# An SSM layer on one core: the first decays' arithmetic moved up, z in half blocks, evictions and residual adds given priority

## The chip, the cores and the metric

The kernel runs as one program on one core of a Trainium2 chip. The metric is the device time of one execution in microseconds (us), a median over several runs. The engines are named as in the profile: PE is the matmul engine and PEld its weight loads, DVE the vector engine, ACT the scalar (activation) engine, POOL the general engine, SP the engine whose queue issues most of the transfers. Matmuls read SBUF and write PSUM, which has eight banks here; a bank can be written again only when what lay in it has been read out.

## The reference, cut to what matters

A two-layer encoder works on 256 prompt tokens and 8 streams of 16 tokens, so 384 tokens of width 1024. Layer 0 is a short convolution beside attention, then a feed-forward block with a convolution. Layer 1, which the change is about, is a state-space (SSM) mixer, followed by another feed-forward block. Its core:

```python
proj = h @ w_in
z, xbc, dt_raw = jnp.split(proj, [D_INNER, D_INNER + CONV_DIM], axis=-1)
xbc, new_conv = causal_dwconv(xbc, conv_state, conv_w, conv_b)
xbc = jax.nn.silu(xbc)
xs, bm, cm = jnp.split(xbc, ...)
dt = jax.nn.softplus(dt_raw + dt_bias);  a = -jnp.exp(a_log)
...
cum = jnp.cumsum(dtc * a, axis=2)
decay = jnp.exp(jnp.where(tri, cum[q] - cum[s], -jnp.inf))
mix = cb[..., None] * decay * dtc            # cb = C B^T within a chunk
y_intra = jnp.einsum('bcqsgr,bcsgrp->bcqgrp', mix, xc)
...
y = (y + d_skip * xs) * jax.nn.silu(z)
y = rms_norm(y in 4 groups, norm_w);  out = y @ w_out;  x = x + out
```

There are 32 heads of 64 in 4 groups, a state of 128, and a convolution over 4 tokens.

## The kernel before, in words

Every product is made of three matmuls (`three`, line 421): weights and activations are each split into a high and a low part, and high x high, high x low and low x high are added in one PSUM bank. The weights come as a stream of tiles of 128 x 1024 in the order of their use. `Weights.take` (line 385) hands out the next columns, and has the tile after the current one made: a transfer on SP's queue, a copy on ACT (`wh`, the high part), a subtraction on DVE (`wl`, the low part). Each of raw, `wh` and `wl` has three buffers, so a tile's `wh` waits until the matmuls of the tile three before it are done.

In the SSM layer PSUM's banks are shared out as three for products (`pmm`) and five for the rest (`paux`). The channels x, B and C come out of `conv4` (line 938) one tile of 128 channels at a time: 24 matmuls of 384 columns into a `pmm` bank (`xbc`), the eviction into `pad` as two DVE multiplications by the norm's factor `R` (lines 946 and 947: 256 and 128 columns), then one ACT and three DVE steps of the convolution (`c`) and a Silu on ACT.

The layer then works through four groups g. `Group.within` (line 1083) makes the states `S` and the part of y within a chunk: per block b a matmul pair `S`, which needs `xw` (POOL, from the turned x), and 32 small matmuls `y`, which need `xdt` (DVE, from the turned x) and the decays `td`. The turned x, `xt`, is x transposed on PE and copied out by ACT, three copies (`turn_x`, line 1006). `decays` (line 1019) is a generator in two parts: the first issues four transfers that spread the cumulated sums over the partitions; the second, after its `yield`, runs 16 Relus and 4 exponentials on ACT. `Group.__init__` (line 1040) multiplies each of the four results by `CB` on DVE.

`project_z` (line 1137) makes z for 512 channels: three `pmm` banks, one for each 128 tokens, over eight slices (kt) of the input width; it is a generator with one step for each three matmuls of 512 columns, 24 steps in all, which the main loop spreads between other work (`steps`). Two kts make one weight tile. `add_out` (line 1197) makes the output projection of the group before: eight products `op` of twelve matmuls, two for each weight tile, each in a `pmm` bank, and each added to the residual stream X by DVE (`residual`, line 518).

What sets the order: all of it is straight-line code. On PE the instructions of this layer keep the order in which they are written (`T.keep`). On the other engines the framework chooses each engine's order when it compiles: it runs a timing model and takes, among the instructions that the model holds ready, the one with the best priority. Priority is the order of writing, except that what is written under `tc.high_priority()` is treated as if it stood at the start of the program. So before the change these go ahead: the making of weight tiles, the `CB` products, the copy of `S` (named `S0` in the code), the adds of y, the scaling of `yi`, and the copies of the turned y. The order is then fixed, and on the chip each engine runs its queue strictly in that order.

Of the kernel before, what the change touches and what calls it, by code (L numbers as in the profile page):

```python
# [14 lines left out]
ALU = mybir.AluOpType  # L15
# [5 lines left out]
KT = 8  # L21
# [209 lines left out]
def build(nc, tc, d, stop=None):  # L231
# [35 lines left out]
    def pmm(name):  # L267
        return psum["mm"].tile([P, 512], F32, tag="mm", name=name)

    def paux(name):  # L270
        return psum["aux"].tile([P, 512], F32, tag="aux", name=name)
# [11 lines left out]
    def prc(name, i):  # L283
        o = COL[name] + i
        return prm[:, o:o + 1]
# [6 lines left out]
    R = cp.tile([P, NT], F32, name="R")  # L292
# [6 lines left out]
    def tt(out, a, b, op, eng=None):  # L299
        (eng or V).tensor_tensor(out=out, in0=a, in1=b, op=op)  # L300

    def stt(out, a, s, b, op0, op1):
        V.scalar_tensor_tensor(out=out, in0=a, scalar=s, in1=b, op0=op0, op1=op1)  # L303

    def act(out, a, f, **kw):
        S.activation(out, a, f, **kw)  # L306
# [92 lines left out]
    W = Weights()  # L399
# [21 lines left out]
    def three(out, ah, al, bh, bl, start, stop):  # L421
        T.matmul(out, lhsT=ah, rhs=bh, start=start, stop=False)
        T.matmul(out, lhsT=ah, rhs=bl, start=False, stop=False)
        T.matmul(out, lhsT=al, rhs=bh, start=False, stop=stop)
# [3 lines left out]
    def run(gen):  # L428
        while True:
            try:  # L430
                next(gen)
            except StopIteration as e:
                return e.value
# [15 lines left out]
    def fm_group(ps, mh, ml, kts, start=True, stop=True):  # L449

        kts = list(kts)
        for i, kt in enumerate(kts):
            wh, wl = W.take()
            three(ps[:, :NT], wh, wl, mh[:, kt, :], ml[:, kt, :],
                  start and i == 0, stop and i == len(kts) - 1)
            yield

    def tm_group(name):

        ps = [pmm(f"{name}{b}") for b in range(3)]  # L460
        for kt in range(KT):
            wh, wl = W.take(512)
            for b in range(3):
                o = slice(b * P, (b + 1) * P)
                three(ps[b], Hh[:, kt, o], Hl[:, kt, o], wh, wl, kt == 0, kt == KT - 1)
                yield
        return ps
# [3 lines left out]
    def small_group(w, n, name, pool):  # L471


        ps = paux(name)
        for kt in range(KT):
            strip = slice(32 * (kt % 4), 32 * (kt % 4) + 32)
            T.matmul(ps[strip, :NT], lhsT=w[:, kt, :], rhs=X[:, kt, :], start=kt < 4, stop=kt >= 4)
        t = pool.tile([P, NT], F32, tag="sq", name=name + "s", bufs=2)
        act(t, ps[:, :NT], AF.Copy)
        ps = paux(name + "t")  # L480
        for b in range(3):
            T.matmul(ps[:, b * n:(b + 1) * n], lhsT=t[:, b * P:(b + 1) * P], rhs=C("hsel")[:, 0:n], start=True, stop=True)
        return ps


    def norm_tile(kt, gain, layer, pool):
        g = prc(gain, 8 * layer + kt)
        act(Hh[:, kt, :], X[:, kt, :], AF.Copy, scale=g)
        stt(Hl[:, kt, :], X[:, kt, :], g, f32(Hh[:, kt, :]), ALU.mult, ALU.subtract)
        if kt == 0:  # L490
            act(acc, X[:, kt, :], AF.Square)
        else:
            sq = pool.tile([P, NT], F32, tag="sq", name="sq", bufs=2)
            act(sq, X[:, kt, :], AF.Square)
            tt(acc, acc, sq, ALU.add)
# [22 lines left out]
    def residual(mt, ps):  # L518
        tt(X[:, mt, :], X[:, mt, :], ps[:, :NT], ALU.add)

    def tok_s(ap):
        return ap.rearrange("p (b t) -> p b t", t=LB)

    def padded(t, w):

        return t[:, 0:w + 256], t[:, w + 256:w + 256 + NB * (LB + w)].rearrange("p (b t) -> p b t", t=LB + w)
# [18 lines left out]
    ps = paux("warm")  # L545
# [55 lines left out]
    def to_features(src, name, fill=None):  # L601

        ps = paux(name)
        for i in range(4):
            T.transpose(ps[:, i * P:(i + 1) * P], src[:, i * P:(i + 1) * P], ident)
        if fill:
            fill(4)
        return ps.rearrange("p (k t) -> p k t", t=P)


    ps = small_group(wsm[:, 0], 8, "f", e1)
# [9 lines left out]
    ps = paux("lfT")  # L621
# [19 lines left out]
    for b in range(3):  # L641
        ps = to_features(q[:, b, :], "qT")
# [8 lines left out]
    for b in range(3):  # L651
        ps = to_features(k[:, b, :], "kT")
# [4 lines left out]
    ps = run(tm_group("v"))  # L657
# [125 lines left out]
    for b0 in range(0, NB, 3):  # L783
        nb = min(3, NB - b0)
        ps = paux("ss")
# [29 lines left out]
    ps = paux("pn")  # L815
# [7 lines left out]
    for j in range(2):  # L823
# [14 lines left out]
        ps = paux("aoT")  # L838
# [12 lines left out]
    for m0 in (0, 4):  # L851
        ps = ops if m0 == 0 else [pmm("op") for _ in range(4)]
# [82 lines left out]
    def t512(tag, bufs=2, shape=(P, 512)):  # L935
        return o1.tile(list(shape), F32, tag=tag, name=tag + "_", bufs=bufs)

    def conv4(i, out):

        ps = pmm("xbc")  # L940
        yield from fm_group(ps, Hh, Hl, range(KT))
        pad = o1.tile([P, 411], F32, tag="pad", name="pad4")
        pp_, ps_ = padded(pad, 3)
        G.memset(pp_[:, 0:3], 0.0)
        G.tensor_copy(ps_[:, :, 0:3], sts[:, i])
        tt(pp_[:, 3:], ps[:, 0:256], R[:, 0:256], ALU.mult)
        tt(ps_[:, :, 3:], tok_s(ps[:, 256:384]), tok_s(R[:, 256:384]), ALU.mult)
        G.tensor_copy(osm[:, i, 0:3], pp_[:, 256:259])
        G.tensor_copy(osm[:, i, 3:27].rearrange("p (b t) -> p b t", t=3), ps_[:, :, 16:19])
        c = o1.tile([P, 411], F32, tag="c", name="c4")  # L950
        act(c[:, 0:408], pad[:, 0:408], AF.Identity, scale=prc("cvs", i), bias=prc("cvsb", i))
        for t in (1, 2, 3):
            stt(c[:, 0:408], pad[:, t:408 + t], prc("cvs", 24 * t + i), c[:, 0:408], ALU.mult, ALU.add)
        act(out[:, 0:256], c[:, 0:256], AF.Silu)
        act(tok_s(out[:, 256:384]), c[:, 259:411].rearrange("p (b t) -> p b t", t=19)[:, :, 0:16], AF.Silu)


    ps = small_group(wsm[:, 1], 32, "dt", o1)
# [11 lines left out]
    def conv_x(g, i):  # L970
        out = t512("xf", 4, (P, NT))
        run(conv4(4 * g + i, out))
        return out

    def conv_bc(which, g):
        out = t512("BC"[which], 1 + which, (P, NT))
        run(conv4(16 + 4 * which + g, out))
        return out
# [158 lines left out]
    def project_z():  # L1137

        ps = [pmm(f"z{b}") for b in range(3)]
        for k0 in (0, 4):  # L1140
            ws = [W.take(512) for _ in range(4)]
            for b in range(3):
                o = slice(b * P, (b + 1) * P)
                for i, (wh, wl) in enumerate(ws):
                    three(ps[b], Hh[:, k0 + i, o], Hl[:, k0 + i, o], wh, wl, k0 + i == 0, k0 + i == KT - 1)
                    yield
        zs = t512("zs", 1, (P, 3, 512))
        for b in range(3):
            act(zs[:, b, :], ps[b], AF.Silu, scale=r[:, b:b + 1])
        return zs  # L1150
# [46 lines left out]
    def add_out(yh, yl, factor):  # L1197
        for m0 in range(0, 8, 2):
            ws = [W.take(256) for _ in range(4)]
            for m in range(2):  # L1200
                ps = pmm("op")
                for kt in range(4):
                    wh, wl = ws[kt]
                    o = slice(m * P, (m + 1) * P)
                    three(ps[:, :NT], wh[:, o], wl[:, o], yh[kt], yl[kt], kt == 0, kt == 3)
                    yield
                if factor is None:
                    residual(m0 + m, ps)
                else:
                    o = t512("xdt", 3, (P, NT))  # L1210
                    tt(o, ps[:, :NT], factor, ALU.mult)
                    tt(X[:, m0 + m, :], X[:, m0 + m, :], o, ALU.add)
                    norm_tile(m0 + m, "g_ffn", 1, o1)
# [15 lines left out]
    bc_ = turn_bc(0, Bn, Cn)  # L1229
    xs.append(conv_x(0, 3))  # L1230
    ps = paux("cT")
# [9 lines left out]
    ps = paux("E")  # L1241
# [11 lines left out]
    decs = decays(0)  # L1253
    next(decs)
    Bn, Cn = conv_bc(0, 1), conv_bc(1, 1)
    nx = [conv_x(1, 0)]
    tjd = t512("h0", 8, (P, 32, LB))
    tt(tjd, dA[:, 64:96].unsqueeze(2).broadcast_to([P, 32, LB]),
       C("Tj").unsqueeze(1).broadcast_to([P, 32, LB]), ALU.mult)
    ps = paux("sgS")  # L1260
# [1 line left out]
    act(decS, ps, AF.Exp)  # L1262

    xt = turn_x(xs)
    grp = Group(0, run(decs), bc_)
    grp.take(xt)
    xs = [*nx, conv_x(1, 1), conv_x(1, 2)]
    grp.skip()
# [1 line left out]
    for g in range(4):  # L1270
# [3 lines left out]
        if gate:  # L1274
            for b in range(3):
                gate.turn(b)
            op = add_out(*gate.y2, None)
        if last:
            break
        decs = run(decays(g + 1))  # L1280
        xs.append(conv_x(g + 1, len(xs)))
        grp.inter(1)
        bc_ = turn_bc(g + 1, Bn, Cn)
# [22 lines left out]
        grp = nxt  # L1306
# [22 lines left out]
    steps(op)  # L1329
    nc.gpsimd.dma_start(out=d["o_sm"], in_=osm)  # L1330
    run(add_out(*gate.y2, gate.factor()))
    T.keep = False
    r = norm_factor(o1)
# [22 lines left out]
```

## Time and profile before

| | |
|---|---|
| time, median of 3 runs | 1062.48 us (1061.84 to 1063.17) |
| time of the profiled execution | 1065.19 us |
| its span (first to last instruction) | 1063.4 us |
| SSM layer's groups, in the span | about 490 to 780 us |
| PE busy in the span | 1039.9 us (98%) |
| DVE, ACT, POOL busy | 739.8, 511.6, 104.4 us |

Times in a row of the profile count from the start of the span. A timeline's row gives the start, the length, the engine, the line, the operation with output and inputs, and a count; in brackets stands the idle time of the engine before it and what ended that. Most lines are those of helpers: L300 is a DVE tensor-tensor operation, L303 a DVE scalar-tensor-tensor, L306 an ACT activation, L240 a matmul.

### The profile page before, as it was taken

The page shows a single profiled execution, that of the slowest core. Times are in us where ns is not written, and L with a number is a line of the kernel's source. Part 1 is how long each engine was busy: PE and PEld are TensorE (multiplying, and loading weights), DVE is VectorE, ACT ScalarE, POOL GpSimd, SP SyncE. Part 2 cuts the span into 40 slices and gives each one's busy share as a digit, 9 for nine tenths or more (in the row PEclk, how much of TensorE's full clock was granted, in tenths as well). Part 3 has the DMA queues.
Part 4 walks back from the last instruction along what each step waited for, and adds up shares of the span by engine and source line. Part 5 has one row for each costly group of instructions (what it writes and reads, how often), then busy time and mean ns, then how long its engine had stood idle before and what let it go on. Part 6 is the DMA issues. An engine that isn't in the chain of part 4 may idle for free.

```text
span 1063.4 us, 16718 instructions
## 1 busy us (share of the span) xinstructions
PE 1039.9 (98%) x6316; PEld 969.7 (91%) x6316; DVE 739.8 (70%) x1361; ACT 511.6 (48%) x855; POOL 104.4 (10%) x339
## 2 busy tenths in 40 slices
PE   9999999999999999999899999899999999999998
PEld 6788799999999999989678888787989999999998
DVE  6967657777777734458989979868987776665331
ACT  5444335444444433346968668364544444443221
POOL 0030010100000000013313112210001100000000
PEclk9999999999999999999999999999999999999999
DMA  7542434344343443435555463553533434434541
GB/s 261 170 158 81 160 112 128 126 122 137 119 132 127 130 136 119 126 108 167 188 187 190 159 198 130 190 179 103 179 125 120 127 120 123 133 122 135 151 136 43
DMA packets 50329, 150.31 MB, mean 141 GB/s; under 512 B 5992, under 2 KB 8312, under 8 KB 50248
## 3 DMA queue, kind: packets, MB, share of 16 engines
q1 hardware_dynamic: 44360, 136.78, 40.9%
q10 hardware_dynamic: 4608, 8.39, 2.1%
q0 software_dynamic: 1280, 4.06, 1.0%
q8 instruction: 50, 0.82, 0.3%
q14 instruction: 31, 0.25, 0.1%
HBM read 135.81 MB, written 13.40 MB: 140 GB/s over the span
## 4 chain that ended last, share of the span: by engine, by line
PE 38%; DVE 13%; ACT 3%; issue 2%; DMA 0%; ACTq 0%; DVEq 0%
PE fg L240 9%; PE fd L240 9%; PE fa L240 8%; PE z L240 4%; PE xbc L240 3%; DVE wl L300 2%; DVE c L303 2%; PE op L240 2%; DVE wl L303 1%; DVE X L300 1%; ACT wh L306 1%; PE y L240 1%; DVE pad L300 1%; PE S L240 0%; ACT L306 0%
## 5 line engine op out<-in xcount | busy, mean ns | idle before, releaser
L300 DVE TENSOR_TENSOR wl<-raw,wh 128x1024 fp32r<-128x1024 f32 (+1 forms) x205 | 252.5, 1232 | 140.6 <-ACT wh L306 140.1
L306 ACT ACTIVATE wh<-raw 128x1024 fp32r<-128x1024 f32 (+1 forms) x205 | 216.0, 1054 | 225.0 <-PE fd L240 95.0
L240 PE MATMUL fg<-Hh,wh 128*128 128x384 f32 x352 | 119.0, 338 | 1.0 <-DVE pad L300 1.0
L240 PE MATMUL fa<-Hl,wh 128*128 128x384 f32 x352 | 119.3, 339 | 0.6 <-DVE Hl L303 0.6
L240 PE MATMUL fg<-Hl,wh 128*128 128x384 f32 x352 | 119.2, 339 | 0.0
L240 PE MATMUL fa<-Hh,wl 128*128 128x384 f32 x352 | 119.0, 338 | 0.0
L240 PE MATMUL fg<-Hh,wl 128*128 128x384 f32 x352 | 119.0, 338 | 0.0
L240 PE MATMUL fa<-Hh,wh 128*128 128x384 f32 x352 | 118.9, 338 | 0.0
L240 PE MATMUL fd<-hh,wh 128*128 128x384 f32 x352 | 118.3, 336 | 0.0
L240 PE MATMUL fd<-hh,wl 128*128 128x384 f32 x352 | 118.3, 336 | 0.0
L240 PE MATMUL fd<-hl,wh 128*128 128x384 f32 x352 | 118.3, 336 | 0.0
L303 DVE SCALAR_TENSOR_TENSOR c<-pad,prm,c 128x400 f32<-128x400 f32 (+1 forms) x160 | 101.9, 645 | 7.9 <-ACT c L306 6.2
L240 PEld LDWEIGHTS fg<-Hh,wh 128*128 128x128 f32 x352 | 66.2, 188 | 1.3 <-ACT R L306 1.3
L240 PEld LDWEIGHTS fa<-Hl,wh 128*128 128x128 f32 x352 | 66.1, 188 | 1.1 <-DVE Hl L303 0.9
L240 PE MATMUL xbc<-Hh,wh 128*128 128x384 f32 x192 | 65.9, 343 | 0.7 <-DVE X L300 0.7
L240 PEld LDWEIGHTS fa<-Hh,wl 128*128 128x128 f32 x352 | 66.2, 188 | 0.1
L240 PEld LDWEIGHTS fg<-Hl,wh 128*128 128x128 f32 x352 | 66.2, 188 | 0.1
L240 PEld LDWEIGHTS fg<-Hh,wl 128*128 128x128 f32 x352 | 66.2, 188 | 0.1
L240 PEld LDWEIGHTS fa<-Hh,wh 128*128 128x128 f32 x352 | 66.1, 188 | 0.1
L240 PEld LDWEIGHTS fd<-hh,wh 128*128 128x128 f32 x352 | 66.2, 188 | 0.0
L240 PEld LDWEIGHTS fd<-hl,wh 128*128 128x128 f32 x352 | 66.2, 188 | 0.0
L240 PEld LDWEIGHTS fd<-hh,wl 128*128 128x128 f32 x352 | 66.2, 188 | 0.0
(737 smaller groups left out, 2108.1 us busy)
## 6 DMA issues: line engine op xcount, KB each, us to landing
raw<-w SPq DMA_DIRECT2D x219, 512.0 KB, 3.5
kc<-kc SPq DMA_DIRECT2D x8, 256.0 KB, 3.5
vc<-vc SPq DMA_DIRECT2D x8, 256.0 KB, 3.0
X<-x SPq DMA_DIRECT2D x8, 192.0 KB, 4.7
o_y<-X SPq DMA_DIRECT2D x8, 192.0 KB, 2.8
o_v<-vt POOLq DMA_DIRECT2D x3, 256.0 KB, 2.5
o_k<-kraw POOLq DMA_DIRECT2D x3, 256.0 KB, 3.3
cst<-cst SPq DMA_DIRECT2D x1, 617.0 KB, 5.9
```

The lines of the kernel that those rows point to most:

```text
L240: ins = nc.tensor.matmul(*a, **kw)
L300: (eng or V).tensor_tensor(out=out, in0=a, in1=b, op=op)
L303: V.scalar_tensor_tensor(out=out, in0=a, scalar=s, in1=b, op0=op0, op1=op1)
L306: S.activation(out, a, f, **kw)
```

## The change

Four edits, no work added or removed:

1. The two DVE multiplications that evict a channel's PSUM bank into `pad` are written under high priority.
2. z is computed in four blocks of two kts instead of two blocks of four: in each, the three banks in turn take six matmuls instead of twelve, and the weights are taken for two kts at a time. The number of steps and of matmuls is the same.
3. The add of an output product to X is written under high priority, where the product needs no factor (the first three groups; the last one's has a factor and is unchanged).
4. For group 0, the second part of `decays` (16 Relus, 4 exponentials) is run right after the first channel of the next group, ahead of the product `tjd`, the exponential `decS` and the turning of x, instead of behind them.

```diff
@@ conv4 @@
-        tt(pp_[:, 3:], ps[:, 0:256], R[:, 0:256], ALU.mult)
-        tt(ps_[:, :, 3:], tok_s(ps[:, 256:384]), tok_s(R[:, 256:384]), ALU.mult)
+        with tc.high_priority():
+            tt(pp_[:, 3:], ps[:, 0:256], R[:, 0:256], ALU.mult)
+            tt(ps_[:, :, 3:], tok_s(ps[:, 256:384]), tok_s(R[:, 256:384]), ALU.mult)
@@ project_z @@
-        for k0 in (0, 4):
-            ws = [W.take(512) for _ in range(4)]
+        for k0 in range(0, KT, 2):
+            ws = [W.take(512) for _ in range(2)]
             for b in range(3):
                 o = slice(b * P, (b + 1) * P)
                 for i, (wh, wl) in enumerate(ws):
@@ add_out @@
                 if factor is None:
-                    residual(m0 + m, ps)
+                    with tc.high_priority():
+                        residual(m0 + m, ps)
@@ main @@
     nx = [conv_x(1, 0)]
+    decs = run(decs)
     tjd = t512("h0", 8, (P, 32, LB))
...
     xt = turn_x(xs)
-    grp = Group(0, run(decs), bc_)
+    grp = Group(0, decs, bc_)
```

## The prediction

> **What bounds the kernel now.** I read the share of busy time first, then PE's waits in the SSM layer, then the load of the other engines and the granted clock there, and last the timelines around the longest waits.
>
> ```profile
> PE 1039.9 (98%) x6316; PEld 969.7 (91%) x6316; DVE 739.8 (70%) x1361; ACT 511.6 (48%) x855; POOL 104.4 (10%) x339
> ```
>
> PE sets the time: whatever is to be won is PE's idle time, and the time in which it runs at a lower clock. No matmul is removed, so the whole question is how many of PE's waits in this layer go. They are these (the columns are total, number, longest):
>
> ```profile
> PE y L240 <- DVE td__4915 L300: 4.6, 1, 4.6
> PE op L240 <- DVE X L300: 3.8, 1, 3.8
> PE z L240 <- DVE wl L300: 1.6, 2, 0.9
> PE z L240 <- ACT wh L306: 1.0, 2, 0.7
> PE fa L240 <- DVE Hl L303: 0.6, 1, 0.6
> PE z L240 <- DVE pad L300: 0.5, 1, 0.5
> PE op L240 <- DVE pad L300: 0.5, 1, 0.5
> ```
>
> Each edit has its rows: the decays (td) 4.6, the residual add (X) 3.8, z's weights 2.6, the evictions (pad) 1.0; 12.0 us in all. The row fa is the feed-forward block behind the layer and stays. The next view gives stretches of the layer: length, then busy time of PE, PEld, DVE, ACT and POOL, the granted clock, and the transfers.
>
> ```profile
> 490.00:545.00 55.00, 50.37 (x354) 42.62 (x353) 49.81 (x84) 47.77 (x98) 17.42 (x41) 0.97 0.49 159
> 560.00:610.00 50.00, 49.52 (x361) 42.88 (x360) 47.84 (x90) 36.56 (x75) 12.00 (x29) 1.00 0.52 173
> 640.00:681.00 41.00, 37.50 (x295) 32.31 (x294) 39.94 (x70) 28.08 (x58) 12.85 (x25) 1.00 0.53 180
> 522.00:527.00 5.00, 4.29 (x53) 2.83 (x55) 5.00 (x9) 5.00 (x12) 0.00 (x0) 0.66 0.52 184
> 683.00:687.00 4.00, 4.00 (x16) 2.09 (x15) 0.75 (x2) 1.06 (x1) 0.00 (x0) 0.57 0.04 10
> ```
>
> Two things are to be seen. DVE is nearly full in three stretches (5.2, 2.2 and 1.1 us idle), and PE's long waits for DVE lie in the first and the third of them. And the two longest waits are each followed by a low clock: 5.00 x (1 - 0.66) = 1.7 us and 4.00 x (1 - 0.57) = 1.7 us are lost, beside the idle time. At most 12.0 + 3.4 = 15.4 us can be won.
>
> **The residual add (edit 3).** The matmul that waits, and DVE's queue before it:
>
> ```profile
> 681.75 0.45 PE L240 MATMUL op<-yh,wh 128*128 128x384 f32 x1 [3.78 <-DVE X L300]
> ```
>
> ```profile
> 680.04 1.19 DVE L303 SCALAR_TENSOR_TENSOR c<-pad,prm,c 128x408 f32<-128x408 f32 x2
> 681.15 1.47 DVE L300 TENSOR_TENSOR X<-X,op 128x384 f32<-128x384 f32 x3
> ```
>
> Three residual adds stand in one block behind convolution steps that were written earlier; the fourth product needs the bank of the first. With high priority each add goes in DVE's next slot after its product, so the first bank is free about three products before it is wanted. Gain 3.8, and the clock's 1.7 with it: 5.5 us. What the adds are put in front of, 0.5 us each, are convolution steps whose Silus feed a transposition that PE reaches only after a whole z (72 matmuls, 17 us at the 0.24 us found below): nothing on the path. Lower bound 0 (the model puts them where they were), upper 5.5; I take 5.5. The next thing due is z, which needs the banks of these products, free by the same edit.
>
> **The evictions (edit 1).** 0.5 at z and 0.5 at op: each waits for a bank whose eviction is queued. Gain 1.0. Cost: 0.6 us of evictions ahead of a wl or a td; a weight tile lasts one channel, 24 matmuls, and is made one tile early, which covers that. Bounds 0 and 1.0; I take 1.0.
>
> **z by two kts (edit 2).** The later of the two z's that wait, and what stands in ACT's queue ahead of the late wh:
>
> ```profile
> 605.68 0.48 PE L240 MATMUL z<-wh,Hh 128*128 128x512 f32 x1 [0.48 <-DVE pad L300]
> ...
> 616.43 0.50 PE L240 MATMUL z<-wh,Hh 128*128 128x512 f32 x1 [0.71 <-ACT wh L306]
> ```
>
> ```profile
> 614.81 0.62 ACT L306 ACTIVATE xf__6125<-c 128x256 f32<-128x256 f32 x2 [3.24 <-DVE c L303]
> 615.33 1.04 ACT L306 ACTIVATE wh<-raw 128x1024 fp32r<-128x1024 f32 x1
> ```
>
> The z's fourth tile takes the buffer of its first. In blocks of four kts the first tile is held until the tenth of twelve steps, and the fourth is wanted at the fifteenth: four steps of three matmuls. In that time wh and wl have to be made, and here wh stood behind a Silu that waited 3.24 us. The 42 matmuls ahead of the late one ran from 605.68 to 615.7 (616.43 less 0.71), 0.24 us each, so four steps are 2.9 us. In blocks of two kts the first tile is free after the sixth step and the fourth is wanted at the nineteenth: twelve steps, 8.6 us. The other tiles come free earlier or at the same step and are wanted at the same step or later. Gain 2.6 us, lower bound 0 (wh still behind the Silu), and a cost only if turning from bank to bank every six matmuls costs something, where every twelve did not show it; I take 2.6. No instruction is added.
>
> **The decays (edit 4).** PE, ACT and POOL, in that order, around the wait:
>
> ```profile
> 517.06 1.02 PE L240 MATMUL S<-xw__5113,Bt__4840 128*128 128x512 f32 x2
> 522.71 1.08 PE L240 MATMUL y<-xdt__5111,td__4915 128*64 128x64 f32 x16 [4.63 <-DVE td__4915 L300]
> ```
>
> ```profile
> 508.76 1.28 ACT L306 ACT_TABLE_LOAD   x1
> 510.06 0.60 ACT L306 ACTIVATE decS<-sgS 128x512 f32<-128x512 f32 x1
> 510.55 0.72 ACT L306 ACTIVATE c<-pad,prm 128x408 f32<-128x408 f32 x1
> 511.17 1.56 ACT L306 ACTIVATE xt__5066<-xT 128x512 f32<-128x512 f32 x3
> ...
> 516.05 1.28 ACT L306 ACT_TABLE_LOAD   x1
> 517.65 0.42 ACT L306 ACTIVATE xf__5015<-c 128x256 f32<-128x256 f32 x1 [0.32 <-DVE c L303]
> 517.98 1.04 ACT L306 ACTIVATE wh<-raw 128x1024 fp32r<-128x1024 f32 x1
> 518.92 0.58 ACT L306 ACTIVATE S__5242<-S 128x512 f32<-128x512 f32 x1
> ...
> 520.01 1.28 ACT L306 ACT_TABLE_LOAD   x1
> 521.30 0.63 ACT L306 ACTIVATE td__4915<-td__4915 128x512 f32<-128x512 f32 x1
> ...
> 522.88 0.61 ACT L306 ACTIVATE td__4921<-td__4921 128x512 f32<-128x512 f32 x1
> ```
>
> ```profile
> 511.85 1.04 POOL L300 TENSOR_TENSOR xw__5113<-xt__5066,wdt 128x512 f32<-128x512 f32 x1 [1.77 <-ACT xt__5066 L306]
> ```
>
> ACT works through from 508.76 to 523.5 with 0.32 us idle, so the wait for td is ACT's backlog, and moving the exponentials up moves something else down: the three copies xt, on which S (through xw) and y (through xdt) hang. Of the 14.7 us, two table loads (2 x 1.28) go if decS and the four exponentials run side by side, and behind the first xt may fall the wh of 517.98 (1.04), the copy of S (0.5 net) and two of three xt copies (1.0). That leaves the first xt at 523.5 - 2.6 - 1.04 - 0.5 - 1.0 = 518.4, xw at 519.4 (1.04 on POOL), S done 1.0 later, y at 520.4 instead of 522.7: 2.3 us won, with the wait now ahead of S (519.4 instead of 517.1) and only 2.3 us long. Upper bound: the whole 4.6 and the clock's 1.7. Lower bound: a Silu falls between the exponentials and the number of loads grows by a pair rather than shrinking, 2 x 2.6 later than 520.4, so 2.9 lost. I take 2.3, being what ACT's own work allows. Whether a wait of 2.3 us still brings the low clock no row shows: 0.9 did not, 3.8 did. I count half of 1.7, 0.9. Sum 3.2. The four transfers of decays are in its first part and stay where they are on SP's queue.
>
> The Trainium skill's "TensorE: Matmul & The Clock Gate" (Why this matters for your kernels) says to allow no idle gaps over about 3 us, since one idle window puts the clock back to half; by it the 2.3 us would keep the full clock and the sum would be 0.8 better. The trace agrees at 3.8 us.
>
> The skill's "ScalarE: Activation LUTs" (What ACT_TABLE_LOAD costs) gives a switch as the load of 1283 ns and a drain of about 1380 ns; the trace has the load at 1.28, but the exponential behind that of 520.01 starts at 521.30, so no drain shows. By the page the two loads saved would be worth 5.3 instead of 2.6, and the measurement decides.
>
> **What is given back.** The lead of 3.2 from the decays and about 1.1 from the earlier z, 4.3 us, reaches the stretch 560 to 610, where DVE has 2.2 us of idle time. DVE gets no less work, so I let what goes beyond that, 2.1 us, be lost to new short waits there. The 5.5 us of edit 3 fall after the full stretches and are kept.
>
> **Sum:** 5.5 + 1.0 + 2.6 + 3.2 - 2.1 = 10.2 us. The profiled execution took 1065.19 us, 2.7 above the median of the runs shown; its waits are taken as those of the other runs, and the gain is taken from the median: 1062.5 - 10.2 = 1052.3 us.
>
> **Rivals.**
> - *The first wait only changes its name* (S waits for xw as long as y did for td, because Silus fall among the exponentials). For it: ACT has no idle time there. Against: two loads can go. Then 5.5 + 1.0 + 2.6 = 9.1, less 1.7, somewhat over half of the lower bound's 2.9: 1055.1 us.
> - *DVE becomes the bound.* For it: 47.84 busy of 50 us. Against: the 8.5 us of idle time in the three stretches, and 30% over the span. PE keeps only what comes behind the full stretches, half of edit 3 and half of z: 4.0; 1058.5 us.
> - *The priorities do little*: the order comes from a model, and if that has the adds ready late, they stay where they are. Then 2.6 + 3.2 + 1.0 = 6.8, less the same 2.1: 4.7; 1057.8 us.
> - *Slower: DVE blocked by its own head.* The rows of DVE's groups in the layer (busy, mean ns, then idle before them):
>
> ```profile
> L300 DVE TENSOR_TENSOR X<-X,op 128x384 f32<-128x384 f32 x24 | 12.9, 543 | 2.2 <-PE op L240 2.2
> L300 DVE TENSOR_TENSOR pad<-xbc,R 128x256 f32<-128x256 f32 x21 | 8.7, 414 | 2.1 <-PE xbc L240 1.5 <-DMA rows<-cumQ 0.5
> ```
>
> The 45 instructions now go as soon as the model thinks their product done. Where PE is later than the model, DVE stands, and wl, td and c behind it stand too. Now that costs 3.7 us in all. In the three full stretches DVE has 8.5 us idle; of the 45 I put 30 there, as an estimate. At 0.6 us each, 18 us, the excess of 9.5 lands on PE, and only 5.5 + 2.6 = 8.1 stands against it, since the decays run through the same queue: 1062.5 + 9.5 - 8.1 = 1063.9 us. It decides from 0.55 us each.
>
> **Chances.** Forecast 0.50 (its own range 1049 to 1055.5), first wait renamed 0.17, DVE bound 0.13, priorities do little 0.10, slower 0.10. A difference under 0.2%, 2.1 us, can't be told from none: the slower case is half within that, and of the two before it a seventh. Faster 0.86, same 0.08, slower 0.06. The range goes from 1048 (all waits gone, 15.4 won, would be 1047.1) to 1061.
>
> **What would show it.** Right: no wait of PE for X above 0.5 us and no clock below 0.9 near 680; z with no wait for wh or wl; the first y 2 us or more earlier against S's channel before it, with one table load less or two between the first Relu and the last exponential. Wrong: a wait of S for xw of 4 us; a clock still at 0.66 near 520; DVE idle before pad or X of 10 us and more; new waits of PE for wl, td or y between 560 and 610.

## The result

The changed kernel took 1056.63 us (median of four runs, 1055.97 to 1057.63) against 1062.21 us (1061.84 to 1063.17): a ratio of 0.9947, interval 0.9930 to 0.9964. It is 5.6 us faster, where 10.2 were forecast. The same two programs on another chip gave 0.9965 (0.9950 to 0.9980), 3.7 us by the ratio.

The profile after. First PE's waits in the SSM layer (total, number, longest):

```profile
PE S L240 <- POOL xw__5113 L300: 2.3, 1, 2.3
PE yT L245 <- DVE y__5780 L300: 2.1, 3, 0.9
PE E L240 <- DVE h__4900 L300: 1.1, 1, 1.1
PE cT L240 <- DVE dA L303: 1.0, 1, 1.0
...
PE yi L240 <- ACT S__5791 L306: 0.8, 1, 0.8
PE y L240 <- DVE xdt__5111 L300: 0.4, 1, 0.4
...
PE op L240 <- DVE X L300: 0.3, 1, 0.3
```

The waits for X (3.8), for z's wh and wl (2.6) and for td (4.6) are gone, as forecast. Four kinds of wait have come: S for xw, yT for y, yi for the copy of S, and cT and E for dA and what is made of it. (The rows left out belong to the feed-forward block. dA is dt times a; cT and E are the small matmuls that sum it up, and h__4900 is dA masked by stream. yi is the part of y that comes from the state, and yT the transposition of the finished y.) Next the stretches of the changed kernel (length, then busy time of PE, PEld, DVE, ACT, POOL, granted clock, transfers):

```profile
490.00:545.00 55.00, 51.16 (x340) 43.08 (x340) 45.56 (x71) 45.43 (x92) 16.64 (x35) 0.91 0.47 150
560.00:610.00 50.00, 47.05 (x345) 39.96 (x343) 48.32 (x90) 35.47 (x78) 14.15 (x29) 1.00 0.53 176
...
493.00:497.00 4.00, 4.00 (x16) 3.97 (x15) 1.10 (x4) 2.50 (x4) 0.77 (x4) 0.58 0.81 285
520.00:528.00 8.00, 7.41 (x80) 4.77 (x82) 7.58 (x10) 6.07 (x17) 4.75 (x5) 0.57 0.41 134
683.00:687.00 4.00, 4.00 (x19) 3.23 (x18) 4.00 (x7) 1.04 (x4) 0.00 (x0) 1.00 0.56 163
```

The clock behind the residual add is full again (1.00 from 683 to 687, where it was 0.57). Near 520 the low clock now costs twice as much: 8.00 x (1 - 0.57) = 3.4 us are lost, which is 6.8 us at half clock, where it was 1.7 us lost or 3.4 us at half clock. A new stretch of it stands at 493 to 497. PE's idle time between 560 and 610 rose from 0.48 to 2.95 us.

Where it went along the layer can be read from the times of single rows. Both traces are lined up at the layer's first PE row:

```profile
463.59 0.61 PE L240 MATMUL ss<-cst,acc 128*128 128x1 f32 x5
```

```profile
460.26 0.72 PE L240 MATMUL ss<-cst,acc 128*128 128x1 f32 x6
```

The first is of before, the second of the changed kernel. A lead is how much earlier a row comes, counted from its own ss row. For example the first y: 522.71 - 463.59 = 59.12 before, 521.93 - 460.26 = 61.67 after, a lead of -2.55. The steps between such rows are the ledger of the layer:

| stretch of PE's work | lead at its end | gained in it | what happens there |
|---|---|---|---|
| to the channel behind E | -2.41 | -2.4 | new waits for dA |
| to the product sgS | -3.98 | -1.6 | new stretch of half clock |
| to the first S | -6.43 | -2.4 | new wait for xw |
| to the first y | -2.55 | +3.9 | the wait for td is gone |
| to the first z | -3.61 | -1.1 | a longer stretch of half clock |
| to the second group's S | -1.87 | +1.7 | z's waits gone |
| to that group's second yi product | -5.33 | -3.5 | new waits of yi and yT |
| to the third stretch of op products | -3.47 | +1.9 | z's waits gone, second z |
| to the z behind the residual add | +2.02 | +5.5 | the wait for X and its half clock gone |

So the layer is 2.0 us shorter in this pair of profiles. The profiled executions differ by 1065.19 - 1056.25 = 8.9 us; the other 6.9 lie ahead of the layer (3.3: 463.59 against 460.26; no edit touches what runs there, and the layer starts between 460.3 and 463.6 us in all the profiles of this case) and behind it, where the profile of before ran the second feed-forward block's rising half 3.5 us slower (190.3 against 186.8 us from its first fa to its first fd). Another profile of before, below, took 187.0 there, so that is a thing of one execution and no part of the change.

### The profile page after: what moved, and what is told of

The parts are those of the page before. It is cut to its first block, busy times and chain, and to the rows that moved or that the text cites. A ratio compares the mean times of both kernels' runs of the same rounds, so it can differ in the third digit from the quotient of the medians.

```text
span 1054.5 us, 16720 instructions
## 1 busy us (share of the span) xinstructions
PE 1034.7 (98%) x6316; PEld 965.3 (92%) x6316; DVE 741.2 (70%) x1361; ACT 508.9 (48%) x853; POOL 110.7 (10%) x339
## 4 chain that ended last, share of the span: by engine, by line
PE 35%; DVE 15%; ACT 3%; issue 2%; DMA 1%; ACTq 0%; POOL 0%; DVEq 0%
PE fd L240 9%; PE fg L240 9%; PE fa L240 8%; PE z L240 5%; DVE wl L300 2%; DVE c L303 2%; DVE wl L303 1%; PE xbc L240 1%; PE op L240 1%; DVE X L300 1%; ACT wh L306 1%; PE y L240 1%; DVE pad L300 1%; ACT L306 0%; PE S L240 0%
```

## The experiments

Ratios are against the kernel before on the same chip. In kernels with an added first line the line numbers in the rows are one higher.

**The evictions alone, and all but the evictions.** The new waits for dA had been nobody's rival. `only_pads` is edit 1 alone, `no_pads` is edits 2, 3 and 4.

```diff
+        with tc.high_priority():          # only_pads: this edit alone
             tt(pp_[:, 3:], ps[:, 0:256], R[:, 0:256], ALU.mult)
```

> The kernel before with edit 1 alone: channel evictions under high priority. Theory A (the evictions start the convolution steps earlier, and these crowd out the chain that makes dt and dA for the first group): the matmuls cT and E of the first group wait for dA and for its masked copy about 2 us together, as in the changed kernel, perhaps with 1.7 us of half clock behind them, and the stretch of the layer before that gains nothing; the layer, from the matmul ss of its norm to the first matmul of the second feed-forward block (313.9 us in the profile of before), is 2 to 5 us longer. Theory B (the evictions are worth the 1.0 us of waits that they took away, and the waits on dA come from the other edits): no wait on dA over 0.3 us, the layer 0 to 1.5 us shorter. Theory C, on the second feed-forward block (190.3 us from its first matmul to the first of its down projection before, 186.8 after): if its pace hangs on what goes before it, it may be either here, and the time of the runs contains that 3.4 us beside the layer's.

> The changed kernel without edit 1 (edits 2, 3 and 4 alone). Theory A: the waits on dA are gone, and with them 2.4 us of idle time and 1.6 us of half clock; the layer is 311.9 - 4 = about 308 us, the shortest so far; with the second feed-forward block as in the changed kernel the time is about 1052.6 us, with that of before about 1056. Theory B: the waits on dA stay, and z and op wait for evictions again; the layer is 312 to 313 us.

`only_pads`: 1060.6 us, 0.9983 (0.9973 to 0.9992). `no_pads`: 1056.37 us, 0.9946 (0.9933 to 0.9958). PE's waits in the first, then in the second:

```profile
PE op L240 <- DVE X L300: 4.8, 1, 4.8
...
PE cT L240 <- DVE dA L303: 1.4, 1, 1.4
PE E L240 <- DVE h__4900 L300: 1.1, 1, 1.1
PE y L240 <- DVE td__4919 L300: 0.9, 1, 0.9
```

```profile
PE S L240 <- POOL xw__5113 L300: 6.0, 1, 6.0
PE yT L245 <- DVE y__5780 L300: 2.0, 3, 1.2
```

The waits for dA come with the evictions and go with them. DVE's rows show how, first of before, then of the changed kernel:

```profile
479.75 0.83 DVE L303 SCALAR_TENSOR_TENSOR lp<-lp,lr 128x96 f32<-128x96 f32 x3
...
487.12 0.29 DVE L303 SCALAR_TENSOR_TENSOR dA<-dt,ea 128x96 f32<-128x96 f32 x1
487.33 0.94 DVE L300 TENSOR_TENSOR pad<-xbc,R 128x256 f32<-128x256 f32 x3
```

```profile
482.36 0.25 DVE L303 SCALAR_TENSOR_TENSOR lp<-lp,lr 128x96 f32<-128x96 f32 x1
482.52 0.63 DVE L303 SCALAR_TENSOR_TENSOR c<-pad,prm,c 128x408 f32<-128x408 f32 x1
...
483.80 0.41 DVE L300 TENSOR_TENSOR pad<-xbc,R 128x256 f32<-128x256 f32 x1
...
488.86 0.25 DVE L303 SCALAR_TENSOR_TENSOR dA<-dt,ea 128x96 f32<-128x96 f32 x1
```

dA comes 487.12 - 463.59 = 23.5 us into the layer before and 488.86 - 460.26 = 28.6 us in the changed kernel. Evictions that run early make convolution steps (c, 0.63 us) ready early, and these alternate with the short steps (lp, 0.25 us) of the chain that ends in dt and dA; before, three lp still followed each other. From the layer's start to dA, DVE does 14 convolution steps and evicts six channels, where before it did 9 and evicted three. Yet the evictions alone are not slower: by `only_pads`, PE, held up for 2.5 us and by the half clock behind that, arrives later at td and waits 0.9 us there instead of 4.6. Theory A's longer layer did not come: it is 315.0 us, between 313.9 and 316.3 in the two profiles of before, so that this trace doesn't show where the 1.8 us by the ratio come from. Without the evictions, on the other hand, the whole wait for xw shows, 6.0 us, and the layer is 310.9 us instead of the 308 of theory A.

**Before and the full change again**, on that chip, for the spread of single profiles.

> The kernel before once more, for a second profile. If the pace of the second feed-forward block belongs to the program, that block takes 190.3 us again and the start-up's clock may differ; the time is 1062 +- 1 us. If the pace is an accident of one execution, the block takes 186.8 us in some execution of it and times of before spread by 3.4 us, which those shown (1061.84 to 1063.17) do not. The layer is 313.9 us within 0.5 by either, unless a wait near 2 us falls differently into the clock's windows, which is worth 1.7 us.

> The changed kernel once more, on the chip of the others, for a second profile. 1056.6 +- 1 us. If the two half-clock stretches of the layer (3.4 us at the first E, 6.8 us at the first y) belong to the waits there, they come again; if they hang on where the clock's windows fall, one of them may be missing or halved, with 1.7 us for each 3.4 us of half clock.

`before_again` 1061.98 us, 0.9998 (0.9989 to 1.0007); `all_again` 1058.39 us, 0.9965 (0.9950 to 0.9980). The second profile of before has the same waits, but twice the half clock behind two of them: 6.8 us each instead of 3.4. That alone makes its layer 2.4 us longer. The second profile of the changed kernel has its half clock at the same two places, 6.8 us at each (3.4 and 6.8 in the first). Its layer is 312.9 us against the 316.3 of the second profile of before, 3.4 us shorter where the first pair gave 2.0. Leads of a single pair of profiles are therefore good to some 3 us where a half clock lies between, and ratios decide.

**Taking the change apart.** Edits 2 and 3; edit 4 alone; edits 1, 2 and 3.

```diff
+    decs = run(decs)                      # only_decays: this alone;
-    grp = Group(0, run(decs), bc_)        # z_resid and pads_z_resid: without it
+    grp = Group(0, decs, bc_)
```

> Edits 2 and 3 without the evictions (1) and the decays (4). Theory A (the decays' move only renames the first wait: y for td becomes S for xw, 4.6 us against 6.0 in the kernel with edits 2, 3 and 4): as fast as that one or up to 1.5 us faster, 1055 to 1056.5 us where before has 1062.3; PE waits 4.6 us for td, none for X, none for wh and wl. Theory B (the decays are worth the 3.2 us of the prediction): 2 to 3 us slower than with edits 2, 3 and 4, about 1059.

> Edit 4 alone. Theory A: the wait of y for td (4.6) is replaced by one of S for xw of 5 to 6 us, X (3.8) and z's wh and wl (2.6) stay: 1062 to 1063.5 us, no gain. Theory B: 1059 us, with a wait of S of 2.3 us or less.

> Edits 1, 2 and 3, the decays where they were. Theory A (evictions make dA late by 2.5 us and thereby shorten the wait for td to about 1 us; the decays add nothing): waits of cT and E for dA together 2 to 2.5 us, y for td 1 to 1.5 us, no wait of S; 1054 to 1056 us, no slower than the full change. Theory B (the decays are worth 3.2): 2 to 3 us slower than the full change, 1059 to 1061.

| kernel | us | ratio, interval | gain in us by the ratio of 1062 |
|---|---|---|---|
| edits 2, 3 | 1053.67 | 0.9914 (0.9896 to 0.9932) | 9.1 (7.2 to 11.0) |
| edit 4 | 1065.22 | 1.0026 (1.0012 to 1.0040) | -2.8 (-4.2 to -1.3) |
| edits 1, 2, 3 | 1054.15 | 0.9923 (0.9906 to 0.9940) | 8.2 (6.4 to 10.0) |
| edit 1 | 1060.60 | 0.9983 (0.9973 to 0.9992) | 1.8 (0.8 to 2.9) |
| edits 2, 3, 4 | 1056.37 | 0.9946 (0.9933 to 0.9958) | 5.7 (4.5 to 7.1) |

PE's longest waits with edits 2 and 3, then with edit 4 alone:

```profile
PE y L240 <- DVE td__4915 L300: 4.7, 1, 4.7
PE yT L245 <- DVE y__5780 L300: 1.7, 2, 1.2
```

```profile
PE S L240 <- POOL xw__5113 L300: 6.0, 1, 6.0
PE op L240 <- DVE X L300: 3.8, 1, 3.8
```

This settles edit 4: it turns a wait of 4.6 us for td into one of 6.0 us for xw, alone and in company, and costs about 3 us. Theory A expected no gain of it, at most 1063.5 us; at 1065.2 it is a loss, and edits 2 and 3 alone came out 1.3 us below A's range and do better than the whole change. The evictions add nothing to them that can be told: with all three edits PE waits 2.0 us for dA and what is made of it, and 1.2 instead of 4.7 us for td.

**The changed kernel repaired.** ACT's rows of the changed kernel show why xw is late:

```profile
509.47 1.28 ACT L306 ACT_TABLE_LOAD   x1
510.76 0.64 ACT L306 ACTIVATE td__4915<-td__4915 128x512 f32<-128x512 f32 x1
511.30 0.62 ACT L306 ACTIVATE td__4917<-td__4917 128x512 f32<-128x512 f32 x1
511.94 1.28 ACT L306 ACT_TABLE_LOAD   x1
513.23 0.62 ACT L306 ACTIVATE xf__5015<-c 128x256 f32<-128x256 f32 x2
513.75 1.05 ACT L306 ACTIVATE wh<-raw 128x1024 fp32r<-128x1024 f32 x1
514.82 1.28 ACT L306 ACT_TABLE_LOAD   x1
...
517.65 0.58 ACT L306 ACTIVATE xt__5086<-xT 128x512 f32<-128x512 f32 x1
```

A Silu falls between the exponentials, so there are three table loads as before, and the first copy xt comes behind them all, 8.4 us after PE was done with the transpositions (PE's next row starts at 509.29). With edits 2, 3 and 4 it is the same: a Silu among the exponentials, three loads, and xt behind them. In `late_xt_first` the copies xt get high priority, and the first six channels' evictions, those ahead of dA, go back to normal. `late_xt_nodec` is the same with the decays where they were before.

```diff
-            act(xt[:, b, :], ps, AF.Copy)
+            with tc.high_priority():
+                act(xt[:, b, :], ps, AF.Copy)
...
-        with tc.high_priority():
+        with (contextlib.nullcontext() if i in (16, 20, 0, 1, 2, 3) else tc.high_priority()):
```

> The full change with two repairs: the six channels of the first group keep their evictions at normal priority (high only from the next channel on), and the copies xt of the turned x get high priority in ACT's queue. Theory A (late dA comes from those six evictions, S's wait from xt being copied behind the exponentials): no wait of cT or E for dA, S waits under 0.5 us for xw, y waits at most 2 us for td; 4 to 5 us less than the full change, 1051 to 1053 us. Rival (the exponentials and y's sums are DVE's and ACT's full load, whatever the order): the same 4 to 6 us come back at y for td or for xdt, 1056 us.

> Edits 1, 2 and 3 with the six channels of the first group at normal priority and the copies xt first; the decays where they were before. Theory A (edit 4 is bad only because it puts xt behind the exponentials; with xt first it saves a table load and is good): y waits 2 to 3 us for td, 1 to 2 us slower than the same with the decays moved, 1055 us. Rival (moving the decays is worth nothing whatever stands ahead of it, since group 1 takes back any lead): the same 1053.8 within 1 us, with the yT and yi waits near 575 shorter by what y waits longer.

`late_xt_first`: 1053.76 us, 0.9918 (0.9897 to 0.9939). `late_xt_nodec`: 1053.37 us, 0.9925 (0.9913 to 0.9938). The waits of the first, then of the second:

```profile
PE yT L246 <- DVE y__5780 L301: 2.0, 3, 1.3
PE yi L241 <- ACT S__5791 L307: 1.3, 1, 1.3
...
PE y L241 <- DVE td__4917 L301: 0.8, 1, 0.8
PE y L241 <- DVE td__4915 L301: 0.8, 1, 0.8
```

```profile
PE y L241 <- DVE td__4915 L301: 4.3, 1, 4.3
PE yT L246 <- DVE y__5780 L301: 1.6, 2, 1.1
```

With xt first, no wait for dA or xw is left, and the first y comes with a lead of 3.9 us and no half clock behind it. By the ratios that is 3 to 5 us better than the whole change, about as theory A said (its 1051 to 1053 us were 0.8 too low). But the kernel without the decays' move, whose y still waits 4.3 us, takes the same time. The rival was right there: the lead of 4.0 us at the second group's S has shrunk to 0.2 at its second yi, while the other went from 1.0 to -1.0.

**Is it DVE's load that takes the lead back?** `late_xt_light` leaves out one of three convolution steps in the second group's four x channels; `late_xt_pool` does that step on POOL instead.

```diff
-        for t in (1, 2, 3):
+        for t in ((2, 3) if i in (4, 5, 6, 7) else (1, 2, 3)):     # late_xt_light
```

```diff
+            if t == 1 and i in (4, 5, 6, 7):                       # late_xt_pool
+                tmp = t512("h0", 8, (P, 408))
+                G.tensor_scalar(out=tmp, in0=pad[:, 1:409], scalar1=prc("cvs", 24 + i), scalar2=None, op0=ALU.mult)
+                tt(c[:, 0:408], c[:, 0:408], tmp, ALU.add, G)
```

> The repaired full change (first six evictions at normal priority, xt first), and the convolution of the four channels of the second group's x without one of its three multiply-adds on DVE: 4 x 0.6 = 2.4 us less work for DVE between 515 and 560; the output of that group is another. Theory A (the lead of 4 us that the first group has is taken back between 575 and 585 because DVE is full): the waits of yi for S and of yT for y, 3.3 us together, fall to 1.5 us or less, 1051.5 to 1052 us where the repaired one had 1053.8. Rival (they are a chain from the gate's z through y to yT, whose length DVE's load doesn't set): they stay at 3 us and the time within 0.5 us of 1053.8.

> The repaired full change (first six evictions at normal priority, xt first) with all its work: the first multiply-add of the convolution of the second group's four x channels is done on POOL, as a product and a sum, instead of DVE (4 x 0.6 = 2.4 us off DVE; on POOL some 1.2 and 1.3 us each by the 1.04 of xw's 512 columns and the 1.68 of y's). Theory A (DVE's load sets the waits of yi and yT near 575): as with the multiply-add left out, yi waits nothing for S and the time is 1051 to 1052.5 us. Rival (the two POOL steps make each of the four chains about 2 us longer, and what hangs on them, the turned x of the second group, comes late or slows DVE): 1054 to 1056 us, with a wait of PE for c's followers or longer rows on DVE.

`late_xt_light`: 1051.0 us, 0.9903 (0.9889 to 0.9916); its interval overlaps that of the repaired kernel, so the time alone decides nothing. In the trace the waits of yi for S (1.3) and of a channel for z's result (0.5) are gone, while yT still waits 2.0. The channel behind yT has a lead of 2.1 us instead of 0.1: the 2.4 us taken off DVE came through to there nearly whole. A stretch of half clock behind yT's waits then cost 1.5 of it. Theory A in its main point, then, though the waits left are 2.0 us and not its 1.5, and the time doesn't settle it.

`late_xt_pool`: 1066.93 us, 1.0052 (1.0038 to 1.0067), slower than before and 11 us above the range of both theories. PE's two longest waits, DVE's group of convolution steps between 500 and 580 (with its idle time), and POOL's rows:

```profile
PE sgS L241 <- DVE h__5083 L301: 6.2, 1, 6.2
PE yi L241 <- DMA h__5225<-h: 3.6, 1, 3.6
```

```profile
L304 DVE SCALAR_TENSOR_TENSOR c<-pad,prm,c 128x408 f32<-128x408 f32 x14 | 9.0, 646 | 12.2 <-POOL c L301 12.2
```

```profile
505.31 2.30 POOL L957 TENSOR_SCALAR h__5056<-pad,prm 128x408 f32<-128x408 f32 x1
...
521.14 3.33 POOL L957 TENSOR_SCALAR h__5166<-pad,prm 128x408 f32<-128x408 f32 x1
524.55 1.05 POOL L301 TENSOR_TENSOR c<-c,h__5166 128x408 f32<-128x408 f32 x1
```

DVE stood 12.2 us at the head of its queue for POOL, and the product sgS, whose operand was queued behind, waited 6.2. The transfers that PE's yi waits for went through buffers that this kernel also uses for the product, so this part is the experiment's own doing.

**Where the half clock comes from.** `no_pads_hold` is edits 2, 3 and 4 with eight more matmuls in the time in which PE stood for xw. They write the bank that S then overwrites.

```diff
+                    if g == 0 and b == 0:
+                        for _ in range(8):
+                            T.matmul(ph[:, 0:384], lhsT=self.Bt[:, b, :], rhs=self.Cg, start=True, stop=True)
                     T.matmul(ph, lhsT=self.Bt[:, b, :], rhs=self.xw[b], start=True, stop=True)
```

> Edits 2, 3 and 4, and in the time in which PE stood 6.0 us for xw eight more matmuls of 384 columns (some 0.77 us each by the 1.02 of a 512-column S, 6.2 us together) into the bank that S then overwrites. All other orders are those of the kernel with edits 2, 3 and 4. Theory A (the half clock behind the wait, 10.2 us long there, comes of PE's idle time): wait for xw under 0.5 us, no stretch of half clock near 520, 5.1 us less work time: 1051 to 1052 us where edits 2, 3 and 4 alone gave 1056.4. Rival B (it comes of the many 64-column products behind, whatever PE did before): the half clock stays, 1056 to 1057 us. The y's are not moved by either, only what follows them, and if DVE is the bound behind 560 (rival C) the 5.1 us come back as waits there: 1055.

1058.7 us, 0.9972 (0.9961 to 0.9984). Stretches of the kernel without the added matmuls, then with them:

```profile
515.00:519.00 4.00, 0.42 (x3) 0.10 (x1) 2.32 (x4) 3.97 (x7) 0.40 (x2) 1.00 0.38 131
519.00:532.00 13.00, 10.16 (x112) 6.12 (x116) 12.43 (x17) 9.29 (x23) 4.91 (x7) 0.61 0.36 115
...
578.00:586.00 8.00, 6.04 (x43) 4.66 (x36) 8.00 (x16) 6.69 (x20) 3.61 (x9) 1.00 0.50 178
```

```profile
515.00:519.00 4.00, 4.00 (x14) 2.35 (x13) 2.84 (x5) 3.99 (x7) 0.40 (x2) 1.00 0.33 123
519.00:532.00 13.00, 10.80 (x135) 6.89 (x134) 13.00 (x18) 10.44 (x26) 5.95 (x8) 1.00 0.38 123
...
578.00:586.00 8.00, 6.35 (x29) 6.12 (x30) 8.00 (x14) 7.98 (x23) 2.73 (x5) 0.79 0.38 132
```

The clock from 519 to 532 goes from 0.61 to 1.00: the half clock is the price of PE's idle time ahead of it, 13 x (1 - 0.61) = 5.1 us of clock here. But the time did not follow. The kernel gained 2.7 us up to the second group's S (lead +0.3 instead of -2.4; not 5.1, since y's first matmul, which waits for xdt, comes no earlier, and only 6.0 of the 10.2 us of half clock lay behind it), and had -5.1 instead of -4.9 at its second yi. Of what it lost there, 1.3 us are longer waits for DVE, which has no idle time from 578 to 586 in both, and 1.7 us are a new stretch of half clock (0.79). Rival C named the place and the direction but 1055 us; the profiled execution took 1056.40, as without the added matmuls (1056.42), and the median is 2.3 us above. The other six executions have a mean granted clock of 0.995 to 0.997 instead of 0.998, worth 1 to 3 us of 1057, so more half clock is at least a part of it; where it lay no profile shows, and why this kernel is slower than the one without the added matmuls, whose executions have 0.994 to 0.995, stays open.

## Why the prediction was right, and where it was not

The time lies in the range and on the side that was forecast, but 4.3 us above the forecast and outside the likeliest case's own range. Two terms of the sum held, one was hidden by another, and one had the wrong sign. Of the signs that the prediction named, those of edits 2 and 3 came; for edit 4 signs of being wrong came: a clock of 0.57 near 520, no table load less and, without the evictions, a wait of S for xw of 6.0 us. That the time is in the range all the same is owed to edits 2 and 3, and to a range that reaches to 1061.

**The residual add (edit 3): 5.5 taken, 5.5 found.** From the third stretch of op products to the z behind the add the lead rises from -3.47 to +2.02 us, the wait and its half clock both. (0.5 of it is the wait of op for pad, counted with edit 1, and 0.3 of the wait for X is left.) What it was moved ahead of cost nothing that shows.

**z by two kts (edit 2): 2.6 taken, 1.7 at the first z and about 2.2 at the second.** No wait for wh or wl is left in any kernel that has the edit. That it came out at more than 2.6 is for 0.2 the shorter wait for the eviction at the second z, counted with edit 1. The rest is a cost that the prediction left out: a wait takes more of PE's time than its own length. The first z of before:

```profile
547.97 0.50 PE L240 MATMUL z<-wh,Hh 128*128 128x512 f32 x1 [0.31 <-ACT wh L306]
549.36 0.50 PE L240 MATMUL z<-wl,Hh 128*128 128x512 f32 x1 [0.89 <-DVE wl L300]
```

The z matmuls start every 0.23 us, each while the one before still runs (0.39 us). From the first of these rows to the second it is 1.39 us, so the wait of 0.89 delayed PE by 1.16. In this z two waits of 1.20 us together cost 1.7. That 1.7 is what comes back later, below.

**The evictions (edit 1): 1.0 taken, with bounds from 0 to 1.0.** The failed step is "a weight tile lasts one channel ..., which covers that": I looked for a cost only in the weights and td behind the evictions, and not in what becomes ready earlier because of them. They bring the convolution steps forward, and those delayed dA by 5.1 us, against which cT had 4.0 us of cover (dA done at 487.41, cT at 491.42 before). The cost is the first two rows of the ledger, 2.4 and 1.6 us. It was largely taken out of the wait for td or xw that followed, so that the edit by itself measured 0.8 to 2.9 us faster, and no gain can be told where the other edits are in.

**The decays (edit 4): 3.2 gained was taken; about 2.8 lost was measured.** The failed step is "two table loads go if decS and the four exponentials run side by side". A Silu was planned between them, there are three loads as before, and xt stands behind the last. xw then took 1.79 us on POOL instead of the 1.04 of its row. That is the rival *the first wait only changes its name*, with its price: its lower bound of 2.9 us is met by the 3.0 us by which the first y comes later with edits 2, 3 and 4. Its time, 1055.1, is 1.5 us below what was measured. The 1057.8 of *the priorities do little* is as near, but its mechanism is not there: the wait for X went. The experiment with xt first shows that the move is not bad in itself, but also that it has nothing to win: with or without it, 1053.8 and 1053.4 us.

**The clock, half of 1.7: mis-sized.** The wait of 2.3 us brought 6.8 us of half clock, 3.4 us of PE's clock, and the two waits of 1.0 and 1.1 us ahead of it another 3.4, or 1.7 us of clock. The Trainium skill's "TensorE: Matmul & The Clock Gate" (Why this matters for your kernels) allows gaps up to about 3 us; by it the forecast would have been 0.8 better, and this trace disagrees with it at 2.3 us.

**What is given back, 2.1: right in place, and in cause as far as `late_xt_light` shows it; too small, and the waits named were others.** I expected wl, td or y. It is yT, which waits until DVE has added the y products out of their banks, and yi for the copy S: 2.9 us of waits near 575 to 581, a lead of 3.5 us lost. In every kernel with edit 2 between 2.0 and 5.4 us are lost at this place; in the three profiles of kernels without it (before again, edit 1, edit 4) nothing is. That z's waits gave DVE the time to catch up there is argued from the rows and not tested: from the first z to the first yT DVE does 36.4 us of work in 41.9 us before, and 36.2 in 40.4 with edits 2 and 3. Nor is DVE busy all that time: with edits 2 and 3 it stands 2.1 and 1.1 us near the end of that z, where the next wl in its queue waits for ACT's wh (0.7 us before). Whether another order there would let the lead through no run shows. As it is, what edit 2 wins at the first z, and any lead of the first group, ends here.

**The sum again, from measured terms:** edits 2 and 3 with what comes back 9.1, edit 4 -2.8, edit 1 between -0.9 (with 2 and 3) and 1.8 (alone): 5.4 to 8.1 us. Measured were 5.6 and 3.7. The rest is within the intervals. The slower rival, DVE blocked by its own head, didn't show its sign, 10 us of idle time before pad or X: it is 6.1 us before pad and none before X in the layer's groups (2.1 and 2.2 before), and DVE's busy time between 560 and 610 rose from 47.84 to 48.32 us. But 4.8 of the 6.1 stand before a single eviction (494.4 to 499.1), in every kernel with all early evictions between 4.8 and 5.5 us; whether anything behind it in the queue was ready then no row shows.

The version to keep is edits 2 and 3 alone: 1053.67 us, two of the four edits, and as fast as the best of the repairs.

## What to carry to other kernels

An edit that moves instructions forward in a queue has to be priced by what becomes ready because of it, not only by what it overtakes: here twelve early evictions filled DVE with convolution steps, and the short chain to dA came 5 us late. A wait that is a backlog is not removed by moving its last operand up; ask what takes the place behind, and test each edit alone: here two of the four made all of the gain, and one of the others was a loss that the sum hid. And a lead is worth only what the next full engine lets through: 4 us won ahead of such a stretch came out as 0.2 us.

## What the runs showed of the hardware

The half clock came in whole stretches of about 3.4 us, one, two or three of them (3.4, 6.8 and 10.2 us in these traces), each 1.7 us of PE's clock (half of 3.4). In time one cost 1.0 to 1.6 us by the leads, and three together 2.7, since a part of them fell on waits. The number varied between executions of one program with the same waits: 3.4 us behind the wait for td in one profile of before, 6.8 in the next. Short waits were not safe: 2.3 us brought two stretches; 1.0 and 1.1 us, 2.3 us apart with only a few small matmuls between, brought one, and 1.4 and 1.1 us there brought two. Single waits of 0.3 to 1.5 us brought none. Three waits of yT, 2.0 us together, brought one stretch in `late_xt_light` and none in `late_xt_first`. POOL's four products of 128x408 with a scalar of each partition took 1.29, 1.30, 2.30 and 3.33 us where its four sums of two tiles of that size took 1.03 to 1.05 us. The spread is not of that operation alone: one xw product of 128x512 took 1.04 us in before and another 2.02 us with edits 2, 3 and 4. One profile ran the second feed-forward block's rising half 3.3 to 3.5 us slower than all the others at full granted clock; what made it so stays open.
